# Stick-breaking attention on one Trainium2 core: the scanned product multiplies differences of successive value rows instead of being turned into weights

## The chip, the cores and the metric

The kernel is one program on one core of a Trainium2 chip. The metric is device time in microseconds (us) of one execution. The kernel before was timed in three runs: 1419.91, 1419.92 and 1420.18 us, median 1419.92 us.

## The reference: what is computed

A residual block over 1024 tokens of width 1024. The change concerns only its attention branch, with 8 heads of width 64:

```
z = q.k / 8;  mask: s < t
log_rem = where(mask, log_sigmoid(z) - z, 0)          # log(1 - sigmoid(z))
between = reverse_cumsum(log_rem) - log_rem
w[t, s] = where(mask, sigmoid(z) * exp(between), 0)
out[t]  = sum over s of w[t, s] * v[s]
```

So a weight is a "stick breaking" share: the sigmoid of its own score times the product of (1 - sigmoid) over the keys between s and t. Around the attention stand a normalisation of the input, one wide projection, a gated linear recurrence (HGRN2), gates, output projections and a squared-ReLU MLP; none of their arithmetic changes.

## The kernel before, in words

**Engines and precision.** All matrix products are made on TensorE from a high and a low part of each operand (`hi_lo`, line 164: ScalarE copies the high part, line 156, VectorE subtracts it for the low part, line 161), mostly in three products (`three`).

**Order of the program.** The program is one stream of Python calls. Matrix work comes from two lanes, "main" (attention) and "fill" (projections and gates that are dealt out between the attention steps, lines 2376 to 2399), so that TensorE always has something to do. A scheduler places each instruction on its engine's list; `after(a, b)` (line 105) is a hint that a is to be issued after b, without a semaphore. Each engine executes its own list strictly in order, and an instruction that waits holds everything behind it on that engine. DMAs are issued by SyncE (SP, most loads; `load`, line 135, chains them in order), by ScalarE (ACT) and by GpSimd (POOL).

**Start of the program.** Two 128-token tiles of x come in, then weights and the other six tiles (lines 2332 to 2343). Each tile is normalised: its mean square is raised to the power -0.5 by POOL (`inv_root`, line 274, for tiles 0 to 3, results `n_0_y` to `n_3_y`; `inv_rms`, lines 265 and 269, for tiles 4 to 7), VectorE multiplies the tile by it (lines 653 and 668), TensorE transposes it (`xnt`, line 131) and ScalarE and VectorE split it (`xnh`, line 348, `xnl`, line 351). Then come the projections of head 0 (`pjqk`) and of all values (`pjv`, 8 token tiles).

**Values.** `v_epilogue` (line 674) splits each tile of 128 value rows straight out of PSUM into `V` (per tile two ScalarE copies and two VectorE subtractions, one for each four heads, lines 678 to 680).

**Attention.** 64 items (8 heads x 8 query blocks of 128, in the order 7, 0, 6, 1, 5, 2, 4, 3). `scores` makes z and two sigmoids of it: `rm` = sigmoid(-z), shifted by one key, line 809, and `bt` = sigmoid(z), line 812; POOL zeroes the last column of `bt` (line 813). `weights` scans `rm` from the right into the running product (line 831; a table `bits` restarts the product at 1 on the diagonal) and multiplies `bt` by it (line 843). `turn` transposes `bt` block by block (`pw`) and splits it into `wTh`, `wTl`; `values` multiplies by V (`po`) and copies the result to `osb` (line 907).

**A side job on POOL.** `out_weight_sums` (line 1312) builds four sums of blocks of the output weight in DRAM (`tw`), with 32 DMAs of 256 KB issued by POOL: 16 plain copies, 8 that add a block of the weight, 8 that add another `tw`. It is a generator; one DMA is taken per second attention item (line 2383). Each DMA carries the hint `after(..., lastsel[0])` (line 1320), where `lastsel` is the latest of the memsets at line 813. The sums are read first at 712 us (`wout2r`).

Of the kernel before, what the change touches and what calls it, by code (L numbers as in the profile page):

```python
# [8 lines left out]

F32 = mybir.dt.float32  # L10
F32R = mybir.dt.float32r
# [28 lines left out]
def kernel(  # L40
# [52 lines left out]
    def dram(name, shape):  # L93
        return scratch.tile(shape, F32, tag=name, name=name)
# [35 lines left out]
    def transpose(dst, src):  # L130
        return pe(nc.tensor.transpose(dst, src, ident))  # L131
# [32 lines left out]
    def hi_lo(h, l, src):  # L164
        hi_copy(h, src)
        return lo_sub(l, src, h)

    def mul(out, a, b):
        return nc.vector.tensor_tensor(out=out, in0=a, in1=b, op=ALU.mult)  # L169
# [501 lines left out]

    vt, qk, osb = {}, {}, {}

    def v_epilogue(ps, tb):
        for quad in range(2):
            if tb % 2 == 0:
                vt[quad, tb // 2] = slot(f"V{quad}_{tb // 2}", F32R)
            V = vt[quad, tb // 2].rearrange("p (t h s d) -> p t h s d", t=2, h=4, s=2)
            src = ps[:, quad * 256 : (quad + 1) * 256].rearrange("p (h d) -> p h d", h=4)
            hi_lo(V[:, tb % 2, :, 0, :], V[:, tb % 2, :, 1, :], src)  # L680

    def v_stat(h, tb):
        c = ((tb % 2) * 4 + h % 4) * P
# [104 lines left out]
    lastsel, turn_lo = [None], [None]  # L788

    def scores(h, qb):  # L790
        open_block("main")
        nk = (qb + 1) * P
        QH, QL, KS = qk[h]
        bt, rm = slot_n(f"bt{h}_{qb}", nk), slot_n(f"rm{h}_{qb}", nk)
        step = 320 if nk == 640 else 512
        for s0 in range(0, nk, step):
            m = min(nk - s0, step)
            n = max(m, 256)
            z = bank(f"z{h}_{qb}_{s0}")
            for i, Q in enumerate((QH, QL)):  # L800
                matmul(
                    z[:, :n],
                    Q[:, qb * P : (qb + 1) * P],
                    KS[:, s0 : s0 + n],
                    start=i == 0,
                    stop=i == 1,
                )
            c0, e = int(s0 == 0), m - (s0 + m == nk)
            nc.scalar.activation(  # L809
                rm[:, s0 + c0 - 1 : s0 + m - 1], z[:, c0:m], AF.Sigmoid, scale=-0.125  # L810
            )
            nc.scalar.activation(bt[:, s0 : s0 + e], z[:, :e], AF.Sigmoid, scale=0.125)
        lastsel[0] = nc.gpsimd.memset(bt[:, nk - 1 : nk], 0.0)
        zs[h, qb] = (bt, rm)


    bits = cpool.tile([P, 1024], U8, tag="bits", name="bits")
    nc.gpsimd.memset(bits, 0)
    nc.vector.tensor_copy(bits[:, 1024 - P - 1 : 1023], ident)

    def weights(h, qb):

        nk = (qb + 1) * P
        bt, rm = zs[h, qb]
        cut = qb == NT - 1
        parts = ((512, nk - 1), (0, 512)) if cut else ((0, nk - 1),)
        for i, (a, b) in enumerate(parts):
            rr = rm[:, a:b][:, ::-1]  # L830
            sc = nc.vector.tensor_tensor_scan(  # L831
                out=rr,
                data0=rr,
                data1=bits[:, 1024 - nk + a : 1024 - nk + b][:, ::-1],
                initial=rm[:, b : b + 1] if i else 0.0,
                op0=ALU.mult,
                op1=ALU.max,
            )
            if (h, qb) == items[0]:
                after(sc, masked[0])  # L840
            if i == 1 or (qb == 5 and h in (2,)):
                after(sc, turn_lo[0])
            m = mul(bt[:, a:b], bt[:, a:b], rm[:, a:b])
            if qb == 5:
                after(m, turn_lo[0])

    def turn(h, qb, between):

        open_block("main")
        bt, rm = zs.pop((h, qb))  # L850
# [12 lines left out]
        tiles = wTt[h, qc]  # L863
        qs = slice(par * P, (par + 1) * P)
        if par == 0:
            for t in tiles[-1]:
                after(nc.gpsimd.memset(t[:, (nkb - 1) % 4, qs].bitcast(F32), 0.0), lastsel[0])
        order = list(enumerate(tiles))
        for i, (th, tl) in order[::-1] if qb == NT - 1 else order:
            n = min(qb + 1 - 4 * i, 4)  # L870
            if n <= 0:
                continue
            if qb == NT - 1 and i == 0:
                between()
# [15 lines left out]
    def values(h, qc):  # L890
        open_block("main")
        tiles = wTt.pop((h, qc))
        nkb = 2 * qc + 2
        po = bank(f"po{h}_{qc}")[:, 0:256]
        for kb in range(nkb):
            for i in range(2):
                matmul(
                    po,
                    v_stat(h, kb),
                    tiles[kb // 4][i][:, kb % 4, :],  # L900
                    start=kb == 0 and i == 0,
                    stop=kb == nkb - 1 and i == 1,
                )
        if to_come.get(h) is None:
            to_come[h] = NT // 2
            osb[h] = slot(f"osb{h}")
        kept = nc.scalar.copy(osb[h][:, qc * 256 : (qc + 1) * 256], po)
# [404 lines left out]
    def out_weight_sums():  # L1312
        b11, b12, b21, b22 = (out_block(i, j) for i in range(2) for j in range(2))
        plain = ((1, b11), (3, b12), (2, b22), (4, b21))
        summed = ((1, b12), (3, b22), (2, tw[1]), (4, tw[2]))
        for op, ways in ((ALU.bypass, plain), (ALU.add, summed)):
            for i, src in ways:
                for r in range(4):
                    rs = slice(r * P, (r + 1) * P)
                    after(nc.gpsimd.dma_start(tw[i][rs], src[rs], accum_op=op), lastsel[0])  # L1320
                    yield

    def gate_bias(which, cb):
# [1205 lines left out]
```

## Time and profile before

| | |
|---|---|
| median of three runs | 1419.92 us |
| span of the profiled execution | 1418.4 us (its own run time is not listed beside it; the median stands 1.5 us above the span) |
| TensorE (PE) busy | 1408.7 us, 99% |
| VectorE (DVE) busy | 1086.9 us, 77% |
| ScalarE (ACT) busy | 684.9 us, 48% |
| GpSimd (POOL) busy | 147.3 us, 10% |
| granted TensorE clock | 0.999 |

How to read it: the span runs from the first to the last instruction. The profile has a page (busy times, the chain of work that ended last, groups of instructions by line) and answers to questions: a timeline of instructions with what released each from its wait, busy times by stretch of time, waits by engine, and DMA issues with their time to landing. A line such as L156 may be that of a helper, so groups are told apart by tile names.

### The profile page before, as it was taken

The numbers are of one execution on the slowest core, as the hardware profiler recorded it, in microseconds if no ns is written. First come the engines' busy times: TensorE is split into PE (matmuls) and PEld (weight loads), VectorE is DVE, ScalarE is ACT, GpSimd is POOL, SyncE is SP. The second block draws the span as 40 slices with busy tenths as digits, with TensorE's granted clock in tenths as the row PEclk, the third lists the DMA queues.
The fourth block names the chain that finished last, engine by engine and source line by source line (L and its number), as shares of the span: only waits on it lengthen the run. The fifth ranks groups of instructions, "written<-read, shape, count | busy, mean of one in ns | idle before, by whom it ended". The sixth has DMA issues, their size and how long they took to land.

```text
span 1418.4 us, 18800 instructions
## 1 busy us (share of the span) xinstructions
PE 1408.7 (99%) x6848; PEld 1183.6 (83%) x6848; DVE 1086.9 (77%) x1493; ACT 684.9 (48%) x1183; POOL 147.3 (10%) x341
## 2 busy tenths in 40 slices
PE   9999999999999999999999999999999999999998
PEld 7888888888888888888888888888888888888886
DVE  7679988988567888887788897676666657668765
ACT  6356676664243554433344764445444443534343
POOL 3012223210011031000000300000000000000042
PEclk9999999999999999999999999999999999999999
DMA  7124445535135685364585514444446974776725
GB/s 238 30 67 127 105 100 98 107 77 157 59 74 171 224 225 178 126 215 156 162 298 193 186 54 169 163 163 143 137 145 239 353 265 149 279 273 238 278 94 188
DMA packets 163173, 237.72 MB, mean 168 GB/s; under 512 B 26332, under 2 KB 93448, under 8 KB 163080
## 3 DMA queue, kind: packets, MB, share of 16 engines
q1 hardware_dynamic: 146056, 190.37, 40.0%
q0 software_dynamic: 11584, 34.61, 10.0%
q10 hardware_dynamic: 5440, 11.54, 2.3%
q8 instruction: 54, 0.88, 0.3%
q14 instruction: 39, 0.32, 0.1%
HBM read 168.32 MB, written 66.06 MB: 165 GB/s over the span
## 4 chain that ended last, share of the span: by engine, by line
PE 98%; DVE 1%; ACT 0%; POOL 0%; DMA 0%; issue 0%; POOLq 0%; SPq 0%; DVEq 0%
PE pm L128 21%; PE pX L128 9%; PE pW L128 6%; PE pY L128 6%; PE pjqk L128 6%; PE pga L128 4%; PE gX L128 4%; PE gY L128 4%; PE pjf L128 3%; PE pjq L128 3%; PE pys L128 3%; PE pji L128 3%; PE pyh L128 3%; PE pjv L128 3%; PE po L128 3%; PE z L128 2%
## 5 line engine op out<-in xcount | busy, mean ns | idle before, releaser
L156 ACT CAST whid<-w 128x1024 fp32r<-128x1024 f32 x30 | 31.6, 1053 | 154.5 <-PE pm L128 87.4
L831 DVE TENSOR_TENSOR_SCAN rm<-rm,bits 128x511 f32<-128x511 f32 (+7 forms) x72 | 87.3, 1219 | 16.4 <-ACT rm L809 16.4
L128 PE MATMUL pm<-wlod,sh 128*128 128x512 f32 x240 | 93.5, 390 | 0.0
L128 PE MATMUL pm<-whid,sl 128*128 128x512 f32 x240 | 93.4, 389 | 0.0
L128 PE MATMUL pm<-whid,sh 128*128 128x512 f32 x240 | 93.4, 389 | 0.0
L128 PE MATMUL pm<-tl,sh 128*128 128x512 f32 (+1 forms) x210 | 81.3, 387 | 0.0
L128 PE MATMUL pm<-th,sl 128*128 128x512 f32 (+1 forms) x210 | 81.3, 387 | 0.0
L128 PE MATMUL pm<-th,sh 128*128 128x512 f32 (+1 forms) x210 | 81.3, 387 | 0.0
L161 DVE TENSOR_TENSOR wlod<-w,whid 128x1024 fp32r<-128x1024 f32 x30 | 36.7, 1222 | 55.3 <-ACT whid L156 55.3
L161 DVE TENSOR_TENSOR sl<-sa,sh 128x1024 fp32r<-128x1024 f32 x56 | 68.2, 1218 | 0.0
L156 ACT CAST wTh<-pw 128x512 fp32r<-128x512 f32 (+2 forms) x96 | 43.8, 485 | 41.9 <-PE pw L131 41.0
L2148 POOL TENSOR_SCALAR fss<-fss 128x1 f32<-128x1 f32 x8 | 4.5, 561 | 562.0 <-ACT fsc L2143 561.5
L156 ACT CAST sh<-sa 128x1024 fp32r<-128x1024 f32 x56 | 57.2, 1046 | 7.2 <-DMA sa<-ad 7.2
L161 DVE TENSOR_TENSOR wTl<-pw,wTh 128x512 fp32r<-128x512 f32 (+2 forms) x96 | 49.9, 546 | 4.6 <-ACT wTh L156 4.4
L128 PEld LDWEIGHTS pm<-wlod,sh 128*128 128x128 f32 x240 | 45.1, 188 | 10.0 <-DVE wlod L161 0.4
L128 PEld LDWEIGHTS pm<-whid,sh 128*128 128x128 f32 x240 | 45.0, 188 | 9.5
L128 PEld LDWEIGHTS pm<-whid,sl 128*128 128x128 f32 x240 | 45.0, 188 | 9.1
L169 DVE TENSOR_TENSOR bt<-bt,rm 128x511 f32<-128x511 f32 (+7 forms) x72 | 48.9, 684 | 3.5
L809 ACT ACTIVATE rm<-z 128x511 f32<-128x511 f32 (+4 forms) x96 | 48.0, 500 | 5.5 <-PE z L128 2.8
L128 PE MATMUL pX<-sqh,t1l 128*128 128x512 f32 x128 | 49.9, 390 | 0.0
L128 PE MATMUL pX<-sql,t1h 128*128 128x512 f32 x128 | 49.9, 390 | 0.0
L128 PE MATMUL pX<-sqh,t1h 128*128 128x512 f32 x128 | 49.8, 389 | 0.0
(932 smaller groups left out, 4434.8 us busy)
## 6 DMA issues: line engine op xcount, KB each, us to landing
w<-in_w_ff_dram SPq DMA_DIRECT2D x72, 512.0 KB, 4.8
sa<-ad SPq DMA_DIRECT2D x52, 512.0 KB, 6.4
ad<-a SPq DMA_DIRECT2D x32, 256.0 KB, 4.3
ad<-s SPq DMA_DIRECT2D x16, 512.0 KB, 3.3
tw<-in_w_out_dram POOLq DMA_DIRECT2D x24, 256.0 KB, 4.6
pr<-pd SPq DMA_DIRECT2D x10, 512.0 KB, 6.0
x<-in_x_dram SPq DMA_DIRECT2D x8, 512.0 KB, 7.8
xnl<-xnh POOLq DMA_DIRECT2D x8, 512.0 KB, 6.5
```

The costliest lines, as they stand in the source:

```text
L128: return pe(nc.tensor.matmul(*a, **k))
L156: hi_last[0] = after(in_turn("act", nc.scalar.copy(dst, src)), hi_behind[0])
L161: nc.vector.tensor_tensor(out=dst, in0=src, in1=hi.bitcast(F32), op=ALU.subtract),
L169: return nc.vector.tensor_tensor(out=out, in0=a, in1=b, op=ALU.mult)
L809: nc.scalar.activation(rm[:, s0 + c0 - 1 : s0 + m - 1], z[:, c0:m], AF.Sigmoid, scale=-0.125)
L831: sc = nc.vector.tensor_tensor_scan(out=rr, data0=rr, data1=bits[:, 1024 - nk + a : 1024 - nk + b][:, ::-1], initial=rm[:, b : b + 1] if i ...
L2148: nc.gpsimd.tensor_scalar(out=ssq, in0=ssq, scalar1=1.0 / D, scalar2=EPS, op0=ALU.mult, op1=ALU.add)
```

## The change

It uses that w[t, s] is the difference of two neighbouring running products. With P(s) the product of sigmoid(-z) from s to t-1, and 1 beyond, w = P(s+1) - P(s), and summation by parts gives out[t] = v[end of block] + sum of P(s) * (v[s-1] - v[s]). So:

- `scores` makes one sigmoid (`rm`, unshifted); `bt`, its memset and `lastsel` go; `weights` only scans; `turn` transposes `rm`. `bits` is made from an upper triangle.
- The value rows are copied to SBUF (`vr`), a copy shifted down by one row is made by DMA (`vb`: 127 rows issued by ACT, the first row from the tile before issued by POOL), VectorE subtracts, and only then are they split into `V`.
- The last row of each block goes through DRAM (`vends`) to a small table `v_end` in which the head's dimensions lie on partitions, and `values` adds it as a bias in two activations of 128 columns in place of one copy of 256.
- The `tw` DMAs and the memsets of `wTh`, `wTl` lose their hint, because `lastsel` is gone.

```
+    def v_epilogue(ps, tb):
+        t = v_rows[tb] = slot_n(f"vr{tb}", 512)
+        if tb == 0:
+            v_before[0] = slot_n("vb0", 512)
+            nc.gpsimd.memset(v_before[0][0:1], 0.0)
+        in_turn("act", nc.scalar.copy(t, ps))
+        nc.scalar.dma_start(v_before[tb][1:P], t[0 : P - 1])
+        if tb + 1 < NT:
+            v_before[tb + 1] = slot_n(f"vb{tb + 1}", 512)
+            nc.gpsimd.dma_start(v_before[tb + 1][0:1], t[P - 1 : P])
+        nc.gpsimd.dma_start(v_ends[tb : tb + 1], t[P - 1 : P])
+        v_steps_back()
+        v_owed.append(tb)
+        if tb == NT - 1:
+            for i in range(2):
+                ts = slice(4 * i, 4 * i + 4)
+                load(v_end[0:DHS, ts], v_ends[ts].rearrange("t (h d) -> d t h", d=DHS))
+
+    def v_steps_back():
+        while v_owed:
+            tb = v_owed.pop()
+            t, b = v_rows.pop(tb), v_before.pop(tb)
+            in_turn("dve", nc.vector.tensor_tensor(out=b, in0=b, in1=t, op=ALU.subtract))
...
+                src = b[:, quad * 256 : (quad + 1) * 256].rearrange("p (h d) -> p h d", h=4)
+                hi_lo(V[:, tb % 2, :, 0, :], V[:, tb % 2, :, 1, :], src)
...
-            c0, e = int(s0 == 0), m - (s0 + m == nk)
-            nc.scalar.activation(
-                rm[:, s0 + c0 - 1 : s0 + m - 1], z[:, c0:m], AF.Sigmoid, scale=-0.125
-            )
-            nc.scalar.activation(bt[:, s0 : s0 + e], z[:, :e], AF.Sigmoid, scale=0.125)
-        lastsel[0] = nc.gpsimd.memset(bt[:, nk - 1 : nk], 0.0)
-        zs[h, qb] = (bt, rm)
+            nc.scalar.activation(rm[:, s0 : s0 + m], z[:, :m], AF.Sigmoid, scale=-0.125)
...
-            m = mul(bt[:, a:b], bt[:, a:b], rm[:, a:b])
-            if qb == 5:
-                after(m, turn_lo[0])
...
-                after(nc.gpsimd.memset(t[:, (nkb - 1) % 4, qs].bitcast(F32), 0.0), lastsel[0])
+                nc.gpsimd.memset(t[:, (nkb - 1) % 4, qs].bitcast(F32), 0.0)
...
-                transpose(pw[:, kb * P : (kb + 1) * P], bt[:, s0 : s0 + P])
+                transpose(pw[:, kb * P : (kb + 1) * P], rm[:, s0 : s0 + P])
...
-        kept = nc.scalar.copy(osb[h][:, qc * 256 : (qc + 1) * 256], po)
+        for b in range(2):
+            qb = 2 * qc + b
+            kept = nc.scalar.activation(
+                osb[h][:, qb * P : (qb + 1) * P], po[:, b * P : (b + 1) * P], AF.Identity,
+                bias=v_end[:, qb, h : h + 1],
+            )
...
-                    after(nc.gpsimd.dma_start(tw[i][rs], src[rs], accum_op=op), lastsel[0])
+                    nc.gpsimd.dma_start(tw[i][rs], src[rs], accum_op=op)
...
         if i + 2 < len(items):
             st.finish(j_qk[items[min(i + 4, len(items) - 1)][0]])
             scores(*items[i + 2])
+        v_steps_back()
```

How the lists of the engines move, first at POOL at the start of the program. Before, behind the constants (`ones`, `mscr`) stand the powers of the normalisation; `n_0_y` is that of token tile 0:

```order
L1013 MEMSET ones 128x128
L1022 IOTA mscr 128x128
L1023 IOTA mscr 128x128
L274 TENSOR_TENSOR n_0_y<-n_0_ms,expo 128x1
L274 TENSOR_TENSOR n_1_y<-n_1_ms,expo 128x1
L274 TENSOR_TENSOR n_2_y<-n_2_ms,expo 128x1
L274 TENSOR_TENSOR n_3_y<-n_3_ms,expo 128x1
```

In the changed kernel, at the same place:

```order
L1036 MEMSET ones 128x128
masks.py:66 AFFINE_SELECT upper<-upper 128x128
L1343 DMA tw<-in_w_out_dram 128x512 x24
L1343 DMA tw<-tw 128x512
L683 MEMSET vb_482 1x512
L274 TENSOR_TENSOR n_0_y<-n_0_ms,expo 128x1
L1343 DMA tw<-tw 128x512
L274 TENSOR_TENSOR n_1_y<-n_1_ms,expo 128x1
L1343 DMA tw<-tw 128x512 x6
L274 TENSOR_TENSOR n_2_y<-n_2_ms,expo 128x1
L274 TENSOR_TENSOR n_3_y<-n_3_ms,expo 128x1
```

All 32 `tw` DMAs have moved from between the attention items to the head of POOL's list: 25 of them stand ahead of the first power, 32 ahead of the third. At most eight of POOL's DMAs are in flight at once, since each of eight semaphores is waited for before it is used again: the 9th issue waits for the 1st landing, and the last (the 32nd) for the 28th.

Second, ACT where the first value tiles come out of PSUM (`pjv`, with the value products of tiles 0, 1, 2) ahead of the split of the second half of the tokens (`xnh`). Before:

```order
L156 CAST wqk1h_454<-wqk1r_451 128x1024
L156 CAST V_0_473<-pjv_316 128x4x64
L156 CAST V_0_476<-pjv_316 128x4x64
L156 CAST V_0_473<-pjv_321 128x4x64
L156 CAST V_0_476<-pjv_321 128x4x64
L156 CAST V_1_520<-pjv_495 128x4x64
L156 CAST V_1_523<-pjv_495 128x4x64
L348 ACTIVATE xnh_526<-xnt_0_528,prm 128x512
```

In the changed kernel:

```order
L156 CAST wqk1h_462<-wqk1r_459 128x1024
L684 COPY vr_481<-pjv_324 128x512
L685 DMA vb_482<-vr_481 127x512
L684 COPY vr_501<-pjv_329 128x512
L685 DMA vb_486<-vr_501 127x512
L156 CAST V_0_508<-vb_482 128x4x64
L156 CAST V_0_511<-vb_482 128x4x64
L684 COPY vr_539<-pjv_514 128x512
L156 CAST V_0_508<-vb_486 128x4x64
L685 DMA vb_504<-vr_539 127x512
L156 CAST V_0_511<-vb_486 128x4x64
L348 ACTIVATE xnh_550<-xnt_0_552,prm 128x512
```

A tile's two casts into V now read `vb`, so they wait for the landing of the 127-row copy and for VectorE's subtraction; they stand on ACT's list ahead of the eight `xnh`, and the third tile's copy is issued only after the first cast of the second tile.

Third, ACT at the end of the same stage, in the changed kernel, where the last two value tiles are followed by the split of head 1's keys and queries (`KS`, `QH`) and by the first transposed products (`wTh`):

```order
L156 CAST V_3_871<-vb_789 128x4x64
L156 CAST V_3_874<-vb_789 128x4x64
L684 COPY vr_866<-pjv_841 128x512
L835 ACTIVATE rm_6_879<-z_6_0_880 128x512
L685 DMA vb_833<-vr_866 127x512
L835 ACTIVATE rm_6_879<-z_6_512_884 128x384
L156 CAST V_3_871<-vb_833 128x4x64
L156 CAST V_3_874<-vb_833 128x4x64
L156 CAST KS_928<-pjqk_0_901 64x512
L156 CAST QH_926<-pjqk_0_901 64x512
L156 CAST wTh_3_4_944<-pw_7_1_946 128x4x128
```

Before, the casts of these tiles read PSUM; now a copy, a DMA and a subtraction stand between, and the issue of each next 127-row copy stands behind the casts of the tile before. TensorE's list has the same 6298 rows in both kernels.

More of the change, by code (lines that the diff above doesn't have):

```diff
@@ L7 @@
 from concourse._compat import with_exitstack
-from concourse.masks import make_identity
+from concourse.masks import make_identity, make_upper_triangular
 F32 = mybir.dt.float32
@@ L672 @@
     vt, qk, osb = {}, {}, {}
+    v_ends = dram("vends", [NT, 512])
+    v_end = cpool.tile([P, NT, NHS], F32, tag="vend", name="v_end")
+    nc.gpsimd.memset(v_end, 0.0)
+    v_rows, v_before, v_owed = {}, {}, []
     def v_epilogue(ps, tb):
[L675 to L680, printed above, removed]
+        t = v_rows[tb] = slot_n(f"vr{tb}", 512)
[19 more added lines that the diff above has]
+            in_turn("dve", nc.vector.tensor_tensor(out=b, in0=b, in1=t, op=ALU.subtract))
+            for quad in range(2):
+                if tb % 2 == 0:
+                    vt[quad, tb // 2] = slot(f"V{quad}_{tb // 2}", F32R)
+                V = vt[quad, tb // 2].rearrange("p (t h s d) -> p t h s d", t=2, h=4, s=2)
+                src = b[:, quad * 256 : (quad + 1) * 256].rearrange("p (h d) -> p h d", h=4)
+                hi_lo(V[:, tb % 2, :, 0, :], V[:, tb % 2, :, 1, :], src)
     def v_stat(h, tb):
@@ L787 @@
     zs, wTt, seen = {}, {}, {}
-    lastsel, turn_lo = [None], [None]
+    turn_lo = [None]
     def scores(h, qb):
@@ L793, in scores @@
         QH, QL, KS = qk[h]
-        bt, rm = slot_n(f"bt{h}_{qb}", nk), slot_n(f"rm{h}_{qb}", nk)
+        rm = zs[h, qb] = slot_n(f"rm{h}_{qb}", nk)
         step = 320 if nk == 640 else 512
@@ L807, in scores @@
                 )
-            c0, e = int(s0 == 0), m - (s0 + m == nk)
-            nc.scalar.activation(
-                rm[:, s0 + c0 - 1 : s0 + m - 1], z[:, c0:m], AF.Sigmoid, scale=-0.125
-            )
-            nc.scalar.activation(bt[:, s0 : s0 + e], z[:, :e], AF.Sigmoid, scale=0.125)
-        lastsel[0] = nc.gpsimd.memset(bt[:, nk - 1 : nk], 0.0)
-        zs[h, qb] = (bt, rm)
+            nc.scalar.activation(rm[:, s0 : s0 + m], z[:, :m], AF.Sigmoid, scale=-0.125)
     bits = cpool.tile([P, 1024], U8, tag="bits", name="bits")
     nc.gpsimd.memset(bits, 0)
-    nc.vector.tensor_copy(bits[:, 1024 - P - 1 : 1023], ident)
+    upper = slot_n("upper", P)[:, 0:P]
+    make_upper_triangular(nc, upper)
+    nc.vector.tensor_copy(bits[:, 1024 - P :], upper)
     def weights(h, qb):
         nk = (qb + 1) * P
-        bt, rm = zs[h, qb]
-        cut = qb == NT - 1
-        parts = ((512, nk - 1), (0, 512)) if cut else ((0, nk - 1),)
+        rm = zs[h, qb]
+        parts = ((512, nk), (0, 512)) if qb == NT - 1 else ((0, nk),)
         for i, (a, b) in enumerate(parts):
@@ L842, in weights @@
                 after(sc, turn_lo[0])
-            m = mul(bt[:, a:b], bt[:, a:b], rm[:, a:b])
-            if qb == 5:
-                after(m, turn_lo[0])
     def turn(h, qb, between):
         open_block("main")
-        bt, rm = zs.pop((h, qb))
+        rm = zs.pop((h, qb))
         qc, par = qb // 2, qb % 2
```

## The prediction

> **What bounds the kernel now.** I read the page first: span, busy times, the chain that ended last.
>
> ```profile
> span 1418.4 us, 18800 instructions
> ...
> PE 1408.7 (99%) x6848; PEld 1183.6 (83%) x6848; DVE 1086.9 (77%) x1493; ACT 684.9 (48%) x1183; POOL 147.3 (10%) x341
> ...
> PE 98%; DVE 1%; ACT 0%; POOL 0%; DMA 0%; issue 0%; POOLq 0%; SPq 0%; DVEq 0%
> ```
>
> TensorE (PE) is 98% of the chain, so the time is the sum of its products plus whatever makes it wait: 9.7 us now (1418.4 - 1408.7). Next I asked for the busy times by stretch; behind the five engines stand the granted clock, the DMA engines' share and their rate.
>
> ```profile
> core 0: us, PE busy (x) PEld busy (x) DVE busy (x) ACT busy (x) POOL busy (x), PEclk, DMA share, GB/s
> 2.00:25.00 23.00, 22.09 (x133) 19.65 (x134) 18.44 (x40) 16.02 (x35) 4.32 (x10) 1.00 1.05 338
> 16.00:18.00 2.00, 2.00 (x11) 1.60 (x10) 1.76 (x4) 0.00 (x0) 1.03 (x2) 1.00 1.02 408
> 80.00:100.00 20.00, 19.68 (x114) 16.86 (x113) 16.82 (x23) 13.28 (x31) 5.02 (x17) 1.00 0.24 66
> 100.00:320.00 220.00, 220.00 (x1268) 190.52 (x1267) 197.96 (x274) 152.03 (x344) 52.40 (x177) 1.00 0.50 105
> 184.50:185.70 1.20, 1.20 (x7) 1.02 (x7) 1.20 (x2) 0.94 (x4) 0.00 (x0) 1.00 0.78 266
> 300.00:305.00 5.00, 5.00 (x33) 4.37 (x32) 4.26 (x7) 2.42 (x7) 1.18 (x4) 1.00 0.96 132
> ```
>
> In the attention stage PE is busy 19.68 of 20 and 220.00 of 220 us. Whatever is saved there on other engines is worth 0.32 us at most. And from 2 to 25 us the DMA engines are full (share 1.05) with the first loads. So I looked next at how the start hangs together, in the timeline:
>
> ```profile
> 1.91 0.29 POOL masks.py:199 TENSOR_SCALAR_AFFINE_SELECT ident<-ident 128x128 f32<-128x128 f32 x1
> 2.15 0.20 POOL L1013 MEMSET ones<- 128x128 f32 x1
> ...
> 2.25 4.63 PE L128 MATMUL warm<-ident 128*128 128x128 f32 x20 [2.25 <-POOL ident masks.py:199]
> ...
> 5.71 0.56 POOL L274 TENSOR_TENSOR n_y<-n_ms,expo 128x1 f32<-128x1 f32 x1 [2.92 <-DVE n_ms L1289]
> ...
> 7.15 0.73 POOL L274 TENSOR_TENSOR n_y<-n_ms,expo 128x1 f32<-128x1 f32 x1 [0.88 <-DVE n_ms L1289]
> ...
> 15.26 1.77 POOL L274 TENSOR_TENSOR n_y<-n_ms,expo 128x1 f32<-128x1 f32 x2 [7.38 <-DVE n_ms L1289]
> ...
> 16.24 1.58 DVE L668 TENSOR_SCALAR x<-x,n_y 128x1024 f32<-128x1024 f32 x2 [0.17 <-POOL n_y L274]
> ...
> 17.97 1.25 PE L131 MATMUL xnt<-ident,x 128*128 128x128 f32 x10
> ```
>
> POOL's power for tiles 2 and 3 starts at 15.26, VectorE scales the tiles at once (it had waited 0.17 us for it), and PE's transposes follow at 17.97. There is no slack: a power that comes d us later moves PE by d.
>
> **The change part by part.** *Removed and added arithmetic.* The groups that go, and those priced for what comes:
>
> ```profile
> L812 ACT ACTIVATE bt<-z 128x512 f32<-128x512 f32 (+3 forms) x96 | 48.1, 501 | 0.0
> ```
> ```profile
> L169 DVE TENSOR_TENSOR bt<-bt,rm 128x511 f32<-128x511 f32 (+7 forms) x72 | 48.9, 684 | 3.5
> ```
> ```profile
> L907 ACT COPY osb<-po 128x256 f32<-128x256 f32 x32 | 12.1, 378 | 19.0 <-PE po L128 18.9
> ```
>
> 48.1 us leave ACT and 48.9 us VectorE. Eight copies of 128x512 (about 0.6 us, as the 128x512 sigmoids), eight subtractions (0.69, as the product) and 64 short bias activations in place of 32 copies (at most 12.1 us more) come. All of it lies beside the full PE: taken as 0, bounds -0.3 and 0.
>
> *The `tw` DMAs at the head of POOL's list.* Without the hint, 25 of the 32 stand ahead of tile 0's power, 32 ahead of tile 2's. Their issues:
>
> ```profile
> L1320 POOL DMA_DIRECT2D tw<-in_w_out_dram x24: 528/564/1192, 82.9 to 253.4; - x24
> L1320 POOL DMA_DIRECT2D tw<-tw x8: 807/982/1597, 266.3 to 306.9; - x8
> ...
> DMA to landing us min/median/max: 2.9/5.1/7.7
> ```
>
> Issuing alone takes 24 x 0.564 + 8 x 0.982 = 21.4 us. But the list also waits for landings: only eight are out at once, and the 32nd issue waits for the 28th to land. What the engines need for 28 of them: a plain copy of 262 KB ran in the stretch 184.5 to 185.7 at 266 GB/s on a share of 0.78, so 341 GB/s on full engines, 0.77 us each; an adding one in 300 to 305 at 132 GB/s on 0.96, 137 GB/s, 1.91 us each. 16 x 0.77 + 12 x 1.91 = 35.2 us. POOL gets to them at about 3 us (its constants end at 2.35; the new triangle costs a memset and a select like those of `ident` and `ones`, 0.5 us), and data move a microsecond later, from 4 us on. From then to 25 us the same engines also have 21 us of first loads. Bounds for the 28th landing: 4 + 35.2 = 39 us if the loads cost these DMAs nothing, 39 + 21 = 60 if all loads go first. I take 49.5: the loads up to x tile 3, which the power needs as well, are about 10 of the 21 us. With the last issue (0.98) the power starts at 50.5 instead of 15.26: **+35 us** (bounds 25 and 46). PE's work between (7.7 us, from 10.3 to 18) fits into the wait, and tiles 0 and 1 are released some 20 us earlier, so they set nothing. Behind POOL's powers wait VectorE's scaling, the transposes, and with them everything. The memsets of `wTh`, which lost the same hint, stand among DMAs of QH and QL; before, they filled gaps, and I cost them at 0, with 2 us if one holds a QL.
>
> *The value rows' detour.* Before, the V casts of two tiles start as soon as ACT is free, and the split of head 1's keys at 79.24 comes 3.68 us after ACT ran dry, with PE setting the pace:
>
> ```profile
> 29.52 0.36 ACT L156 CAST V<-pjv 128x256 fp32r<-128x256 f32 x1
> ...
> 36.36 4.74 ACT L348 ACTIVATE xnh<-xnt,prm 128x512 fp32r<-128x512 f32 x8
> ```
> ```profile
> 79.24 0.58 ACT L156 CAST KS<-pjqk 64x512 fp32r<-64x512 f32 x1 [3.68 <-PE pjqk L128]
> ```
>
> Now the list of ACT is a chain: copy, 127-row DMA, VectorE's subtraction, casts, and only then the next tile's DMA. Behind a waiting cast stand on ACT the `xnh` that PE's next projection needs, the copies that free PSUM banks, and KS and QH. So the landing time L of the 127-row copy decides. No DMA of 127 rows is in the trace. The nearest rows are ACT's copies of 256 KB:
>
> ```profile
> pd<-p ACTq DMA_DIRECT2D x10, 256.0 KB, 2.1
> ...
> od<-osb ACTq DMA_DIRECT2D x7, 256.0 KB, 2.9
> ```
>
> They have 128 and 64 rows, which 16 engines share evenly. Low bound: L = 2.1 us. High bound: everything on one engine. Sixteen move 408 GB/s in the stretch 16 to 18, one 25.5 GB/s; 127 x 2048 bytes take 10.2 us, plus what of the 2.1 us isn't moving (2.1 - 262/408 = 1.5): L = 11.7; at the plain copies' 341 GB/s it would be 13.7. I take 11.7, though the rows' own time is 2.1: 127 is a prime, so no split in equal shares exists, and the one-row copies on POOL's list are written as 16 pieces of 32 while this one stays 127x512. The Trainium skill, "DMA: Bandwidth & Descriptors", section "Queues, rings and completion order", states that the number of engines is the largest up to 16 that divides the slowest dimension, with 127 partitions as its example of one engine; no trace here shows it, and it speaks for the sum with 11.7 and against the one with 2.1.
>
> The chain: copy of tile 0 ends at 30.2 (29.52 + 0.6). Tile 0 lands after L; tile 1, already queued behind it, 10.2 later; tiles 2 to 7 cost L each, since each issue stands behind the casts before it. Between them (subtraction 0.7, casts 0.37 each, copy 0.6; after tile 3 also KS, QH and a weight split, 2.2; for tile 7 a sigmoid, 0.5) I count 1.1 + 1.1 + 4.3 + 2.05 + 2.05 + 2.6 + 1.45 = 14.65. In all 30.2 + 7 x 11.7 + 10.2 + 14.65 = 137, against 79.24 now: 58 us. PE runs ahead until its banks are full, an estimate of 3 us: **+55 us**; with 13.7 it is 71. With L = 2.1 the chain ends at 60, before 79: hidden by PE, 0. It begins to cost at about L = 4.5. The DMAs that fill `v_end` stand on SyncE's list ahead of the `wga8r` loads; those have their slack from the same delay, 0, with 5 us if they are late.
>
> *Restarts of PE.* After waits of many microseconds PE may start slowly. The warm-up took 4.63 us for 20 products; later ones of that shape:
>
> ```profile
> 35.19 3.49 PE xnt L131 x32
> ```
>
> 0.109 us each, so 20 cost 2.2: the first ones lost 2.4 us, though PEclk shows 1.00. Two restarts are followed by PE-bound work, behind tile 2 and behind the value chain: **+5 us** (bounds 0 and 5).
>
> *Sum.* 35 + 55 + 5 = 95 us. On the profiled execution 1418.4 + 95 = 1513.4; the median stands 1.5 above that span, so **1515 us**.
>
> **Rivals.** *The 127-row copy is spread over the engines.* For it: every 256 KB copy from ACT lands in 2 to 3 us. Against it: none of those has an odd number of rows. Then the detour is hidden, and the start remains: 1419.9 + 35 + 5 = 1460.
>
> *The start isn't held for long.* POOL hands its DMAs over and waits only for issues: 21.4 us of issuing from 3 us on, the power at 24.4 instead of 15.26, +9. For it: 0.56 us per issue. Against it: the re-used semaphores. With the value chain: 1419.9 + 9 + 55 + 3 = 1487.
>
> *Not slower: both streams are hidden by PE's own work.* At the start that needs 32 issues between 3 and 15.26 us, 0.38 us each with no landing waited for, and for the values L below 4.5 us. The first is under the shortest issue seen (0.528), the full DMA engines speak against it too. Beyond that point PE waits; below it the time is 1419.9 - 0.3 = 1419.6, within 0.2%.
>
> **How the numbers follow.** The forecast (both delays, one engine) gets 0.72; the spread copy 0.17, because nothing measured here shows a 127-row copy; the short start 0.06; the hidden one 0.01; 0.04 for worse things unnamed. Low end: the spread copy with the start near its low bound, 1420 + 25 + 5, 1450, so 1452. High end: 46 + 71 + 5 is 1542, and 8 us for QL, `wga8r` and the like: 1550. Outside are the tails of these cases, some 0.15. 0.2% is 2.8 us, about what a measurement of this kernel can tell from no change. Faster: less than 0.01, put at 0.01 with mechanisms not seen; same 0.01; slower 0.98.
>
> **What would show it.** Right: in the profile after, POOL's first power starts after 20 us and the third near 50, both behind `tw` issues; PE idle in the first 50 us; eight ACT DMAs `vb` with a landing near 12 us; ACT's V casts waiting for the `vb` subtraction; KS of head 1 some 90 us later than 79; PE again full from there on. Wrong: `vb` landing near 2 us, the third power before 35 us, or idle time on PE in the attention stage, which would mean that a memset or `v_end` holds something I cost at nothing.

## The result and the profile after

The changed kernel takes 1532.05 us (median of four runs, 1530.95 to 1533.52), the kernel before 1419.91 us beside it (1419.89 to 1420.18): a ratio of 1.079, interval 1.0775 to 1.0805, 112.1 us more. The prediction said 1515 us in a range of 1452 to 1550.

The head of the page after, and its chain of work by engine and line:

```profile
span 1531.5 us, 18626 instructions
...
PE 1425.6 (93%) x6848; PEld 1196.0 (78%) x6848; DVE 1049.4 (69%) x1429; ACT 659.5 (43%) x1127; POOL 151.3 (10%) x296
...
PE   1655589999999999999999999999999999999998
...
PEclk9877889999999999999999999999999999999999
...
PE 87%; DMA 10%; ACT 1%; POOL 1%; issue 0%; DVE 0%; ACTq 0%; POOLq 0%; DVEq 0%
```

PE ran the same 6848 products but waits 105.9 us (1531.5 - 1425.6) instead of 9.7. In the row of 40 slices (38.3 us each) the holes are in the first six, up to about 200 us; behind them PE is as full as before. The rest of the loss, 16.9 us (1425.6 - 1408.7), is PE's own busy time: the granted clock (PEclk) drops in the same slices. DMA, 0% of the chain before, has 10%.

What PE waits for, in the view of waits (total, times, longest); by the digits above nearly all of it lies ahead of 200 us:

```profile
PE xnt L131 <- DVE x L653: 28.5, 2, 28.2
PE pw L131 <- DVE QL L161: 14.2, 1, 14.2
PE xnt L131 <- DVE x L668: 11.7, 2, 11.4
PE z L128 <- DMA QH<-QH: 10.7, 1, 10.7
PE pjv L128 <- DVE xnl L351: 10.5, 1, 10.5
PE pw L131 <- ACT vr L684: 8.7, 1, 8.7
PE xnt L131 <- ACT vr L684: 7.1, 1, 7.1
PE z L128 <- DMA QL<-QL: 5.4, 1, 5.4
```

The two waits for a scaled `x` are the start; the other six lie in the stage of the values. The start first, in POOL's timeline:

```profile
2.78 4.39 POOL L1343 DMA_DIRECT2D tw<-in_w_out_dram  x8
9.91 0.52 POOL L1343 DMA_DIRECT2D tw<-in_w_out_dram  x1 [2.73 <-DMA tw<-in_w_out_dram]
...
34.91 0.57 POOL L274 TENSOR_TENSOR n_y<-n_ms,expo 128x1 f32<-128x1 f32 x1
...
58.14 0.81 POOL L1343 DMA_DIRECT2D tw<-tw  x1 [0.42 <-DMA tw<-tw]
58.69 1.67 POOL L274 TENSOR_TENSOR n_y<-n_ms,expo 128x1 f32<-128x1 f32 x2
```

and the longest piece of the chain of work ahead of that last issue (start, length):

```profile
40.67 17.18 DMA tw<-tw
```

Eight issues go out at once, the ninth waits for a landing, and so on to the last at 58.14. That last one, the 32nd, waits for the 28th landing, at 57.86 (40.67 + 17.18): it adds the block of `tw` that the 28th has just summed. So this wait comes from the data, where the description of the change put it down to the eight semaphores. The first power comes at 34.91 instead of 5.71, the third at 58.69 instead of 15.26: 43.4 us later. Then the values, in ACT's timeline:

```profile
73.72 0.58 ACT L684 COPY vr<-pjv 128x512 f32<-128x512 f32 x1
74.33 1.23 ACTq L685 DMA_DIRECT2D vb<-vr  x1
...
89.22 0.71 ACT L156 CAST V<-vb 128x256 fp32r<-128x256 f32 x2 [13.03 <-DVE vb L701]
...
194.09 0.71 ACT L156 CAST V<-vb 128x256 fp32r<-128x256 f32 x2 [13.72 <-DVE vb L701]
194.83 0.58 ACT L156 CAST KS<-pjqk 64x512 fp32r<-64x512 f32 x1
```

The casts of most tiles wait some 13 us, nearly all of it for the copy `vb`. KS of head 1 comes at 194.83 instead of 79.24, 115.6 us later; that contains the start's 43.4.

And the attention stage behind it, by stretch, in the columns that the prediction shows:

```profile
200.00:360.00 160.00, 160.00 (x918) 138.78 (x918) 119.07 (x153) 90.37 (x208) 26.44 (x76) 0.99 0.32 74
```

PE is busy 160.00 of 160 us. VectorE and ACT are not; what they were spared there buys nothing.

### The profile page after: what moved, and what is told of

Read it like the earlier page. It is cut to its first block, busy times and chain, and to the rows that moved or that the text cites. A ratio compares the mean times of both kernels' runs of the same rounds, so it can differ in the third digit from the quotient of the medians.

```text
span 1531.5 us, 18626 instructions
## 1 busy us (share of the span) xinstructions
PE 1425.6 (93%) x6848; PEld 1196.0 (78%) x6848; DVE 1049.4 (69%) x1429; ACT 659.5 (43%) x1127; POOL 151.3 (10%) x296
## 4 chain that ended last, share of the span: by engine, by line
PE 87%; DMA 10%; ACT 1%; POOL 1%; issue 0%; DVE 0%; ACTq 0%; POOLq 0%; DVEq 0%
PE pm L128 20%; PE pX L128 9%; DMA vb<-vr 6%; PE pW L128 6%; PE pY L128 6%; PE pjqk L128 4%; PE pga L128 4%; PE gX L128 4%; PE gY L128 4%; PE pjf L128 3%; PE pjq L128 3%; PE pys L128 3%; PE pji L128 3%; PE pyh L128 3%; PE po L128 2%; DMA tw<-in_w_out_dram 2%
## 5 line engine op out<-in xcount | busy, mean ns | idle before, releaser
L852 DVE TENSOR_TENSOR_SCAN rm<-rm,bits 128x512 f32<-128x512 f32 (+6 forms) x72 | 87.4, 1222 | 22.9 <-ACT rm L835 21.4
L131 PE MATMUL pw<-ident,rm 128*128 128x128 f32 x288 | 43.9, 276 | 22.8 <-DVE QL L161 14.2
L701 DVE TENSOR_TENSOR vb<-vb,vr 128x512 f32<-128x512 f32 x8 | 5.5, 692 | 83.2 <-DMA vb<-vr 83.2
L131 PEld LDWEIGHTS pw<-ident,rm 128*128 128x128 f32 x288 | 35.9, 143 | 31.1 <-issue 14.6
L131 PE MATMUL xnt<-ident,x 128*128 128x128 f32 x64 | 12.4, 360 | 47.3 <-DVE x L653 28.5
L128 PEld LDWEIGHTS pm<-whid,sh 128*128 128x128 f32 x240 | 45.1, 188 | 9.5
```

What stands on the lines that cost most here:

```text
L128: return pe(nc.tensor.matmul(*a, **k))
L701: in_turn("dve", nc.vector.tensor_tensor(out=b, in0=b, in1=t, op=ALU.subtract))
L852: sc = nc.vector.tensor_tensor_scan(out=rr, data0=rr, data1=bits[:, 1024 - nk + a : 1024 - nk + b][:, ::-1], initial=rm[:, b : b + 1] if i ...
```

## The experiments

Theory: the loss is the sum of two streams of DMAs, the `tw` packets (the 32 DMAs of 256 KB) ahead of POOL's powers and the copy of 127 rows in the value chain. The rivals were that one of them hides the other, that the slow restarts of PE are a part of their own, or that the detour by DMA as such, at any speed, holds the values.

**1. The `tw` packets behind again.**

```
-                    nc.gpsimd.dma_start(tw[i][rs], src[rs], accum_op=op)
+                    after(nc.gpsimd.dma_start(tw[i][rs], src[rs], accum_op=op), held[0] or last_power[0])
```

(`held` is the memset of `wTh` that the change had freed.)

> The changed kernel, with the 32 tw DMAs hinted behind the latest wTh memset again, so that they lie between the attention items on POOL's list. Theory A (POOL's list order makes the start late, and the one-engine copy of the value rows makes the rest): the start returns to that of before (third power near 15 us), the value chain stays; 43 us less than 1532, so 1489 us. Rival B (the new loads and DMAs of the value stage also need the early tw traffic to be slow, one cause with two faces): well below 1480. Rival C (the changed arithmetic itself costs in the attention stage): the same 1489 here, so this run does not tell C from A.

Measured: 1488.70 us, 1.0483 (1.0469 to 1.0497). So the packets cost 43.35 us (1532.05 - 1488.70), nearly what the third power lost (43.43).

**2. The copy in two pieces, 112 and 15 rows.**

```
-        nc.scalar.dma_start(v_before[tb][1:P], t[0 : P - 1])
+        nc.scalar.dma_start(v_before[tb][1:113], t[0:112])
+        nc.scalar.dma_start(v_before[tb][113:P], t[112 : P - 1])
```

> The changed kernel, with each copy of 127 rows issued as two DMAs, of 112 and of 15 rows; the tw DMAs stay at the head of POOL's list. Theory A: 112 rows go to 16 engines and 15 to 15, both land in 2 to 3 us, the value chain disappears behind PE, the start stays late: 1420 + 43 + up to 3 for slow restarts of PE, 1463 to 1466 us, and V casts that hardly wait. Rival B (a copy between two SBUF tiles is slow whatever its rows, or the DMA's fixed cost and the casts behind it make the chain): the landing stays at 8 us or more and the time above 1500.

Measured: 1465.16 us, 1.0316 (1.0302 to 1.0330). The same rows, moved by one more DMA per tile, take 66.9 us less. PE's waits in the stage of the values are gone but for one of 0.9 us, those of the start are nearly all that is left; and the list of DMA issues has a landing of 2.7 us:

```profile
PE xnt L131 <- DVE x L653: 27.7, 2, 26.7
PE xnt L131 <- DVE x L668: 12.0, 2, 11.7
```
```profile
vb<-vr ACTq DMA_DIRECT2D x8, 224.0 KB, 2.7
```

**3. Both edits.**

> The changed kernel with both edits: tw DMAs hinted behind the wTh memsets, and copies of 112 and 15 rows. Theory A: nothing else in the change is on PE's path, 1419 to 1422 us, ratio 1.000 within 0.002. Rival C (bias activations, v_end, memsets ahead of QL, or waits in the value stage cost something): 1424 us or more, with idle time of PE between 30 and 100 us. Rival D (97 us less work on ScalarE and VectorE is worth something): below 1418.

Measured: 1424.59 us, 1.0032 (1.0020 to 1.0045). Nearly all of it comes back, not all: 4.5 us are left (1424.59 - 1420.06), and they don't lie where I had costed nothing out of caution (`v_end`, the memsets) but at one wait of PE, of which ACT's timeline shows the cause:

```profile
PE pjv L128 <- DVE xnl L351: 2.8, 1, 2.8
```
```profile
30.03 0.65 ACTq L685 DMA_DIRECT2D vb<-vr  x1
30.72 1.40 ACTq L686 DMA_DIRECT2D vb<-vr  x1
...
36.38 0.71 ACT L156 CAST V<-vb 128x256 fp32r<-128x256 f32 x2 [3.64 <-DVE vb L702]
...
39.85 4.73 ACT L348 ACTIVATE xnh<-xnt,prm 128x512 fp32r<-128x512 f32 x8
```

The eight `xnh` that PE's next products need start at 39.85 instead of 36.36: six issues and a cast that waits stand ahead of them. The wait is 2.8 of the 4.5 us. The rest is the pace behind it. The 24 products that follow, in the chain of work of the kernel before and of this one:

```profile
38.68 5.47 PE pjv L128 x24
```
```profile
41.37 7.31 PE pjv L128 x24
```

They take 1.84 us more, at a granted clock of 0.55 from 41.3 to 45.1 us where the kernel before has 1.00; 2.8 + 1.8 is 4.6. No run separates the pace from the wait.

**4. Only the `tw` packets, in the kernel before** (the hint taken from that one line; nothing else of the change).

> The kernel before, with nothing changed but the hint of the tw DMAs taken away, so that they go to the head of POOL's list (19 ahead of the first power, all 32 ahead of the third). Theory A: the start is late as in the changed kernel, 43 us and 1 to 3 us of slow restart, 1463 to 1466 us. Rival B (the start of the changed kernel is late for something else in it, such as the new constants on POOL): about 1420.

Measured: 1463.51 us, 1.0307 (1.0291 to 1.0323), 43.45 us more than before. It is the same price with and without the rest of the change, so the packets and the copy of 127 rows add and don't hide each other. With the short copies the packets cost less, 40.57 us (1465.16 - 1424.59): behind the late start PE waits 0.9 us for `xnl` instead of 2.8, so part of the 4.5 us of experiment 3 is hidden there.

**5. Eight of the 32 packets first**, in the kernel with both edits: the plain copies to the first two `tw` slots have no hint, the other 24 keep it.

```
-                    after(nc.gpsimd.dma_start(tw[i][rs], src[rs], accum_op=op), held[0] or last_power[0])
+                    d = nc.gpsimd.dma_start(tw[i][rs], src[rs], accum_op=op)
+                    if op == ALU.add or i in (2, 4):
+                        after(d, held[0] or last_power[0])
```

> Against the run with both edits (1424.6), the first eight of the 32 tw packets (those of the first two tw slots, plain copies without a wait) stand at the head of POOL's list again, the other 24 behind. Theory A: the packets hold the start as transfers that alternate with the first loads, in proportion to their bytes as long as no packet waits for another: 8 of 32 packets, so 8 of the 43.4 us of the whole move divided by four, some 8 to 11 us: 1432 to 1436. Theory B: they hold it by POOL's list, and then by the ninth and later packets' waits for landings (12.2 us at the 29th): eight issues at 0.77 us put the first power 1 to 2 us later and no more: 1425 to 1427. Rival C, nothing: 1424.6.

Measured: 1428.73 us, 1.0062 (1.0049 to 1.0074), 4.1 us more than with none first. That lies between the two theories. POOL's timeline and the list of issues say why:

```profile
2.78 4.41 POOL L1344 DMA_DIRECT2D tw<-in_w_out_dram  x8
...
7.67 1.12 POOL L274 TENSOR_TENSOR n_y<-n_ms,expo 128x1 f32<-128x1 f32 x2
21.92 1.75 POOL L274 TENSOR_TENSOR n_y<-n_ms,expo 128x1 f32<-128x1 f32 x2 [13.13 <-DVE n_ms L1313]
```
```profile
x<-in_x_dram SPq DMA_DIRECT2D x8, 512.0 KB, 13.3
```

POOL's list is clear at 8.8 us and the third power still comes at 21.92, waiting for its input: the tiles of `x` land 13.3 us after their issue, 9.7 in the run with none first. There the power stood at 15.19, so eight packets cost it 6.7 us. Their own time on the DMA engines is 8 x 0.77 = 6.2 us. So a packet that nobody waits for holds the start by about the time that it takes on the engines. The whole kernel loses less, 4.1 us, because the later start again hides part of the detour: PE waits 0.9 us for `xnl` here, 2.8 in experiment 3.

**6. The copy in 124 and 3 rows**, otherwise as with both edits.

> Against the run with both edits, the copies take 124 and 3 rows instead of 112 and 15. Theory A (rows are dealt to as many engines as the largest number up to 16 that divides them: 4 for 124): 31 packets of 84 ns on each of 4 engines, 2.6 us, and the 2.5 us around them: 5.1 us from issue to landing instead of 2.7. Each V tile's subtraction is 2.4 us later, once or twice ahead of xnh: 1427 to 1430. Rival B (124 rows go to 16 engines unevenly): 2.7 us and 1424.6. Rival C (only 127, or any number not divisible by 16, goes to one engine): 13 us, and 1485 to 1492.

Measured: 1439.77 us, 1.0139 (1.0125 to 1.0153). The landing is nearly what theory A said, the time is not. How many engines move a copy can be read from the DMA share of a stretch in which little else runs: one engine of 16 is 0.06. Of the changed kernel, with 127 rows, and of this one:

```profile
165.00:176.00 11.00, 5.59 (x30) 4.43 (x28) 0.00 (x0) 0.00 (x0) 0.14 (x1) 0.99 0.07 23
```
```profile
77.50:81.50 4.00, 4.00 (x19) 3.30 (x18) 0.76 (x2) 0.57 (x2) 0.00 (x0) 1.00 0.26 66
```

0.07 and 23 GB/s: one engine. 0.26 and 66 GB/s: four. In the chain of work (start, length) the 127 rows of the changed kernel stand with 13.2 us, the 124 of this one with 5.5:

```profile
99.62 13.23 DMA vb<-vr
```
```profile
54.85 5.48 DMA vb<-vr
```

The Trainium skill, "DMA: Bandwidth & Descriptors", section "Why a DMA increments its semaphore by 16 and not by 1", states the rule: the largest number up to 16 that divides the slowest dimension, 127 giving one engine; 124 would give four, and the two shares agree. (The prediction named another section of that page for it.)

So 2.8 us more per copy cost 15.2 us, and 7.7 us more cost a further 49 (1488.70 - 1439.77): 5.4 and 6.4 us for each microsecond of landing. The chain through ACT's list has no threshold in these runs: it costs 4.5 us at a landing of 2.7 already and grows from there.

**7 and 8. PE kept warm at the start**: the kernel of experiment 2, whose start is long, with dummy products of the identity in front of the two waits (100 and 40; then 132 and 54).

```
-    keep_warm(1)
+    keep_warm(132)
     norm_transpose(xn, 0, 0, 2, lambda: keep_warm(1))
...
+    open_block("main")
+    keep_warm(54)
     norm_transpose(xn, 0, 2, 2)
```

> Against the run with copies of 112 and 15 rows alone (1465.16, PE idle 27.7 and 12.0 us at the start), dummy products of the identity fill most of both waits (100 and 40 of them, about 0.23 us each), and nothing else is moved. Theory A: each restart costs time, since products ran at half pace for 6.9 us behind the first wait (a 128x256 product every 0.21 us instead of 0.12) and for some 3 us behind the second: 3.4 and 1.5 us, 5 in all, so 1459.5 to 1461.5. Rival B: that half pace is hidden behind DVE and ScalarE, which pace the first products: 1464.5 to 1465.5. Rival C, the dummy products hold the real ones: over 1466.

> As the run with dummy products (1466.18 against 1465.16 without), but with 132 and 54 instead of 100 and 40 of them: those left PE idle for 7.4 and 3.3 us ahead of the first products, and the rows behind each show half pace again (six 128x128 in 1.54 us). Now they reach up to the products. Theory A: the restart at half pace costs 3.4 and 1.5 us: 1460 to 1462, the first six xnt in 0.9 us. Rival B, the pace comes back and the time does not, since DVE and ScalarE pace these stages: 1464 to 1466.5. Rival C, the dummies run beyond the moment at which x is ready and hold the products: over 1467.

Measured: 1466.18 us, 1.0329 (1.0313 to 1.0345), and 1464.40 us, 1.0317 (1.0302 to 1.0333), against 1465.16, 1.0316, without. The smaller numbers left PE idle for 7.4 and 3.3 us just ahead of the products, and its pace was down again. The larger ones did what they should; the stretches around the restarts, without dummies and with 132 and 54:

```profile
34.00:44.00 10.00, 8.74 (x47) 8.27 (x48) 7.47 (x18) 7.56 (x17) 3.14 (x4) 0.65 1.09 289
...
59.00:66.00 7.00, 6.32 (x29) 5.63 (x30) 6.12 (x12) 4.98 (x10) 0.29 (x1) 0.58 0.70 132
```
```profile
36.00:44.00 8.00, 6.67 (x53) 6.12 (x52) 6.73 (x13) 6.49 (x15) 2.83 (x4) 1.00 1.08 290
...
60.00:66.00 6.00, 5.01 (x35) 4.25 (x36) 5.80 (x12) 4.67 (x10) 0.12 (x1) 1.00 0.79 146
```

The granted clock goes from 0.65 and 0.58 to 1.00, and the time moves by 0.8 us, with runs that overlap. (The run with 100 and 40 is 1.0 us slower than the one without, beyond the spread of both; in its profile the third power starts at 58.93 us, 1.3 later than without, and why is not shown.) The Trainium skill, "TensorE: Matmul & The Clock Gate", section "Part 1: The HAM clock gate (the "warmup" mystery)", states that an idle window of about 3.4 us halves the clock; the lowered rows, which stand behind waits of 26.7 and 11.7 us, agree. In experiment 3 the pace was halved behind a wait of only 2.8 us, and there the measurement decides.

The total hides a little. In the profiled executions the third power starts at 57.61 us without dummies and at 58.45 with 132 and 54, and the split of head 0's keys, the first KS, at 70.61 and 70.42: 13.00 us behind the power, then 11.97. So the slow clock costs about 1 us at the second restart, and a power that came 0.8 us later covered it. That it costs no more fits VectorE and ACT, busy 6.73 and 6.49 of 8 us in the stretch at 36: they pace most of these products.

**9. ACT's list cleared**: the kernel with both edits, with the `vb` copies issued by POOL and the subtractions and casts of tiles 0 to 2 behind the `xnh`.

```
-        nc.scalar.dma_start(v_before[tb][1:113], t[0:112])
-        nc.scalar.dma_start(v_before[tb][113:P], t[112 : P - 1])
+        nc.gpsimd.dma_start(v_before[tb][1:113], t[0:112])
+        nc.gpsimd.dma_start(v_before[tb][113:P], t[112 : P - 1])
...
-        v_steps_back()
+        if not turns["on"]:
+            v_steps_back()
         v_owed.append(tb)
...
-            tb = v_owed.pop()
+            tb = v_owed.pop(0)
...
     norm_transpose(xn, 1, 0, 4)
+    v_steps_back()
```

> Both edits of the two runs before are in (tw packets behind, copies of 112 and 15 rows), and ScalarE's list is cleared ahead of tile 1's first xnh: the vb copies are issued by POOL instead of ScalarE, and the subtractions and V casts of tiles 0 to 2 come behind those xnh. Theory A: the 4.5 us that were left (1424.6 against 1420.1) are ScalarE's list ahead of xnh (xnh x8 at 39.85 instead of 36.36, PE waiting 2.8 us for xnl), so xnh goes back to 36.4 to 37 and the time to 1419.5 to 1421. Rival B: the 4.5 us are something else (a transfer in the way, VectorE's longer list, the later osb copies): 1423.5 or more, with xnh early and PE still waiting. No theory gives less than 1419: PE is full from 8 us on.

Measured: 1420.37 us, 1.0004 (0.9995 to 1.0012): the 4.5 us are gone. `xnh` starts even before its old place, right behind the third `vr`, and the casts come behind it, from 42.21 on:

```profile
35.00 0.58 ACT L684 COPY vr<-pjv 128x512 f32<-128x512 f32 x1 [4.67 <-PE pjv L128]
35.48 4.74 ACT L348 ACTIVATE xnh<-xnt,prm 128x512 fp32r<-128x512 f32 x8
```

This is summation by parts with its costs taken out, and it equals the kernel before: PE's sum of products is the floor of both.

**10. Only the issues moved**: as with both edits, the `vb` copies issued by POOL (the first four lines of the diff of experiment 9).

> Only the queue that issues the vb copies is changed against the run with both edits: POOL issues them, ScalarE does not. Theory A splits the 4.5 us: six issues of 0.57 to 1.40 us lie on ScalarE ahead of xnh, 4.9 us in all, but ScalarE also waits 3.64 us there for vb's subtraction, and that wait stays; half of the delay goes: 1421 to 1423, PE's wait for xnl 0.5 to 2 us. Rival B, the V casts alone hold xnh (they wait for the copy, which lands no sooner): 1424 to 1425. Rival C, the issues alone: 1420 to 1421.

Measured: 1423.70 us, 1.0027 (1.0017 to 1.0037; runs from 1421.96 to 1424.62). The move of the issues alone gives about 0.9 us of the 4.5, with intervals that overlap; `xnh` starts at 39.14. The step from here to experiment 9 gives 3.3 us (1423.70 - 1420.37), so what holds `xnh` is mostly the casts' wait for the subtraction.

**11. Three behind instead of one**: the kernel of experiment 1, copy whole and slow, but a tile's subtraction and casts come two tiles later.

```
-        v_steps_back()
+        v_steps_back(2)
...
-    def v_steps_back():
-        while v_owed:
-            tb = v_owed.pop()
+    def v_steps_back(kept=0):
+        while len(v_owed) > kept:
+            tb = v_owed.pop(0)
```

> Against the run with the tw packets behind and the copy left at 127 rows (1488.7), a tile's subtraction and casts come two tiles later than now (three behind instead of one), so ScalarE's list waits less for each copy; the copies themselves are untouched. Theory A: what the slow copy costs is its place in a chain (each V cast waits for its copy, the next vr waits for the cast), and the floor beneath is the one DMA engine: eight copies of 10.7 us, 86 us from 30.6 on, so the last V tile at 117 to 120 instead of 151, KS of head 1 some 38 us behind before's 79: 1450 to 1465. Rival B, the chain stays because the last four tiles still wait one by one: 1475 to 1485. Rival C, the copy's length does not matter and something else holds: 1488.

Measured: 1480.20 us, 1.0424 (1.0410 to 1.0438): 8.5 us won of 68.6. Rival B came: the last tiles still wait one by one, and there is a new stall in ACT's timeline:

```profile
35.64 8.54 ACTq L685 DMA_DIRECT2D vb<-vr  x1
44.23 4.15 ACT L348 ACTIVATE xnh<-xnt,prm 128x512 fp32r<-128x512 f32 x7 [8.02 <-issue]
...
140.60 0.71 ACT L156 CAST V<-vb 128x256 fp32r<-128x256 f32 x2 [10.90 <-DVE vb L701]
```

**12. The 127 rows from POOL's queue**: the kernel of experiment 1 with one word changed.

```
-        nc.scalar.dma_start(v_before[tb][1:P], t[0 : P - 1])
+        nc.gpsimd.dma_start(v_before[tb][1:P], t[0 : P - 1])
```

> As the run with the tw packets behind (1488.7), the copy left whole at 127 rows, but issued by POOL instead of ScalarE: one word of the code. Theory A: what puts 127 rows on one engine belongs to the queue that ScalarE issues on, and POOL's queue deals them to all 16 engines: landing at 2 to 3.5 us and the time of the run with split copies issued by POOL, 1423.7, so 1421 to 1425. The Trainium skill, DMA: Bandwidth & Descriptors, section Why a DMA increments its semaphore by 16 and not by 1, states that on trn2 copies issued by GpSimd can be spread so, with 127 as an example; no run so far shows it. Theory B: 127 rows go to one engine from any queue: landing at 13 us and 1485 to 1491.

Measured: 1424.03 us, 1.0026 (1.0015 to 1.0037). From the list of issues:

```profile
vb<-vr POOLq DMA_DIRECT2D x8, 254.0 KB, 2.8
```

The same copy of 127 rows lands in 2.8 us instead of 13.2, and 64.7 us of 68.6 come back. The Trainium skill, on the page and in the section named in experiment 6, states this exception: on trn2 some copies issued by GpSimd are dealt to 16 engines although the number of rows has no such divisor, with 127 as an example. The run agrees: 254 KB in 2.8 us is some 90 GB/s, where the one engine moved 23 and four moved 66. How many engines took part is not read from this trace.

## Why the prediction was right, and where its sizes were off

*Removed and added arithmetic, 0.* Right. PE is busy 160.00 of 160 us in the attention stage, and experiment 9, with all of the new arithmetic in it, equals the kernel before (0.45 us, the interval spans 1). So the gain on these two engines went nowhere: by the two pages ACT is busy 25.4 us less and VectorE 37.5 us less, beside an engine that has no gap to close.

*Start, 35 us (bounds 25 and 46).* Mechanism right, size 43.4. The step that failed is "the loads up to x tile 3 ... are about 10 of the 21 us", by which the 28th landing came out at 49.5. These stretches of the kernel after stand against it:

```profile
2.00:25.00 23.00, 5.56 (x23) 5.02 (x23) 1.94 (x7) 1.46 (x5) 12.18 (x24) 1.00 1.06 322
25.00:60.00 35.00, 12.69 (x62) 11.25 (x62) 8.85 (x21) 7.89 (x17) 12.78 (x18) 0.90 1.01 228
```

The DMA engines are full from 2 to 60 us, and the 28th landing, which the last issue waits for, is at 57.86. That is close to the upper bound, 4 + 35.2 + 21 = 60: not only the loads that the power needs, but nearly all of the first loads shared the engines with the packets before the 28th was down. Experiments 1 and 4 give the term as 43.35 and 43.45. The rival "the start isn't held for long" falls: the last two powers would have come at 24.4, and experiment 5 shows that packets hold the start even where POOL never waits for one.

*Value rows, 55 us.* One engine, right: the share of 0.07 and the 13.2 us show it, and experiments 2 and 12 spread the same rows and win 66.9 and 64.7 us. The rival of the spread copy would have been right for either of these kernels, not for the one changed. The size is 68.6 (1488.70 - 1420.06; what PE's slow restart costs there is part of it). The term that was mis-sized is L, 11.7. It measured 13.23, nearer to the 13.7 that stood beside it, which makes 7 x 1.53 = 10.7 us of the difference. From the first `vr` to KS of head 1 the chain took 121.1 us (194.83 - 73.72); the prediction's took 107.5 (137 - 29.5). That working leaves 2.9 us. Of these 1.80 is a wait of ACT that the sum has not got: for the sixth tile PE's products `pjv` were late, not the copy. From the chain, with a row of later in the program beside it, and from ACT's timeline:

```profile
140.11 7.88 PE pjv L128 x24
...
673.32 5.44 PE pys L128 x24
```
```profile
148.01 0.59 ACT L684 COPY vr<-pjv 128x512 f32<-128x512 f32 x1 [1.80 <-PE pjv L128]
```

The `pjv` come behind waits of PE of 10.7 and 5.4 us, with a granted clock of 0.50 from 133 to 141 us, and take 2.4 us more than the products at full clock: a slow restart inside the chain. The last copy, with 14.05 us, makes another 0.8.

*"It begins to cost at about L = 4.5."* Wrong, and costed at 0 was what lies below. At L = 2.7 the detour costs 4.5 us (experiment 3), at 5.5 it costs 19.9 (1439.77 - 1419.92). I had asked only whether KS of head 1 at 79.24 would be late. The first thing on ACT's list with no slack stands 40 us earlier: the `xnh` of the second half, at 36.36, which PE needs at once. Experiment 9 moves them ahead of the casts, and the cost is gone.

*Restarts, 5 us.* PE does start slowly after a wait, but the size was off and the place too. At the start, where VectorE and ACT pace the products, it is about 1 us (experiment 8). In the stage of the values PE-bound products follow at once: the 24 products take 2.4 us more in the changed kernel, of which 1.80 reach the chain, and 1.84 more in experiment 3. So experiments 1 and 2 have the restarts within their prices, and no run takes one in the value stage away by itself.

*`v_end` and the memsets, 0.* Right: no wait for them is in PE's list, and experiment 9 leaves no room for one.

Together, with the price of the packets from experiment 4, which has nothing else of the change: 43.45 + 68.64 = 112.1, as measured. Both large terms came out above their forecast, so no error hid another; the sum lay within the range because the bounds allowed for later landings.

## What to carry to other kernels

Look at the number of rows of a DMA and at the queue that issues it before you put it into a chain: the same 127 rows took 13.2 us from ACT and 2.8 us from POOL, and two DMAs of 112 and 15 rows took 2.7. A hint that looks like bookkeeping (an `after` on a transfer for later) may be what keeps a stage clear that has no slack; when a change deletes the instruction that it hangs on, look for what it held. And ask for the first instruction behind a new wait on that engine's list, not only for the one at the end of the chain.

## What the runs showed of the hardware that was not expected

- In the run of experiment 11, ACT's issue of a third copy lasted 8.54 us where the others of it took 0.6 to 1.2, with two copies still on the one engine. ACT does nothing else in that time. That a full queue held it is an argument, no run isolates it.
- In experiment 5, eight transfers on another queue delayed the loads of `x` by about their own time on the engines (6.7 against 6.2 us), although those loads were issued on SyncE and nothing in the start waited for the eight.
- In experiments 3 and 10, PE waits of 2.77 and 2.06 us behind 32 transposes were enough for a slow pace: the next 24 products took 7.31 and 7.36 us instead of 5.47. In experiment 2 a wait of 0.9 us at the same place left them at 5.74.
- Without dummies PE's granted clock stood at 0.58 to 0.65 in the stretches behind the long waits, and 3.3 us of idleness in experiment 7 were enough to bring a slow pace back (13 transposes in 2.97 us, 0.23 each; 0.13 in experiment 8).
